# A hybrid layer on one core: five groups of the seven products in w2 of FFN 2, an order of its own for its last part, and softplus among FFN 1's pair jobs

## The chip, the cores and the metric

The kernel runs on one core of one Trainium2 chip. The metric is the time of one execution on the device in microseconds (us). The times shown are of repeated executions of the whole kernel, and the profile is of one more execution of it.

## The reference, cut to what matters

One layer of a streaming encoder for 512 tokens of 1024 channels, in float32. Two feed-forward networks (FFN 1 and FFN 2, hidden width 2816 = 22 tiles of 128) stand around a mixer (a recurrent branch and an attention branch, merged).

```python
def swiglu(x, w1, w3, w2):
    return (jax.nn.silu(x @ w1) * (x @ w3)) @ w2

f = swiglu(rms_norm(h, ffn1_pre_g), ffn1_w1, ffn1_w3, ffn1_w2)
h = h + 0.5 * rms_norm(f, ffn1_post_g)
u = rms_norm(h, mix_pre_g)
...   # recurrent branch: log_a = -8 * r * softplus(-lam), with r a sigmoid; attention; gates
h = h + rms_norm(merged @ w_o, mix_post_g)
f = swiglu(rms_norm(h, ffn2_pre_g), ffn2_w1, ffn2_w3, ffn2_w2)
h = h + 0.5 * rms_norm(f, ffn2_post_g)
```

## The kernel before, in words

**Arithmetic.** Every float32 operand of a product is split into a high part, rounded to the format that TensorE takes, and a low part, the rest. One product is three matmuls: high by high, high by low, low by high. ScalarE makes the high parts, VectorE most of the low ones (a subtraction: `split2`, line 214; `split_to`, line 179).

**w1 and w3 of an FFN: `Pairs`.** The hidden tiles are made two at a time in jobs ("pair jobs", the `run` of `Pairs`, matmuls in lines 683 to 685). Each job computes a 2x2 block product with seven products instead of eight, on sums and differences of blocks: VectorE and POOL make the sums, VectorE and ScalarE split them. `late` is a table of small tasks that are put at marked places (1, 2, 3) of given jobs. `tail()` in the last job prepares the first units of w2.

**w2 of an FFN: `Halves`.** The 22 hidden tiles are the inner dimension. 16 of them, in four groups of four, are multiplied by the same seven-product scheme over halves of the tokens and of the output columns: the products m1, m5, m2, m6, m7, m3, m4 follow one another, and each runs over the four groups. One product of one group is a "unit", u = 0 to 27: twelve matmuls of 128x512 (lines 615 to 617). `prep` makes a unit's operands: a block of w2 (`raw`) is split into `hi` and `lo`, the hidden values into the two parts of `xs`, and then `sums` makes the differences of blocks (`T`, line 548) and of hidden values (`S`, line 551) for later units. Where the low weights come from depends on the product: for m1, m5, m6, m7, m4 VectorE subtracts (line 596); for m2 ScalarE writes the negative of the high part and a DMA issued by POOL adds the weights from HBM to it (line 594); for m3 the high part itself comes by a casting DMA of POOL (line 602), ScalarE writes its negative (line 587) and a POOL DMA adds the weights (line 588).

At step u the program emits the preparation of unit u + 4 (`LEAD = 5`: all units below u + 5), then the hooks of the step, then the unit's matmuls. The first four units are prepared in the last pair job. The hooks load and split the remaining six tiles and read h back. Products that share banks of PSUM are copied out in between (`out`: ScalarE, line 629, after m1, m5 and m6; VectorE's addition, line 627, after m7).

**The rest of w2: `tok_gemm`.** The six tiles left over (`TAIL`) are multiplied classically (`mm_tok`, lines 242 to 244), token tile by token tile and half by half of the output columns, and each token tile is then normed and stored (`post_norm`): an addition where a part lies in a slot (`part`, line 294), the sum of squares by ScalarE (line 298), the gain (line 299), 1/sqrt, and the output (line 310).

**Buffers and order.** SBUF work tiles come from one pool of `NSLOT = 42` slots of 4 KB a partition, given out in the order of the program, so a request waits until an earlier tile of the pool is done with. Loads of weights are queued on SP, broadcasts and adding DMAs on POOL. Each engine takes its instructions in the order in which the program emits them; TensorE runs through units without pause as long as operands are there.

**softplus.** In step 25 of FFN 1's w2 a hook emits softplus(-lam) and three scaled copies of biases: two operations of ScalarE and 28 small ones of VectorE, on 8 to 40 columns (lines 1126 to 1143).

Of the kernel before, what the change touches and what calls it, by code (L numbers as in the profile page):

```python
# [13 lines left out]
ALU = mybir.AluOpType  # L14
# [37 lines left out]
def hybrid_layer(ctx: ExitStack, tc: tile.TileContext, a: dict, out: bass.AP):  # L52
# [65 lines left out]
    want("w2a", TAIL)  # L118
# [16 lines left out]
    want("w2b", TAIL)  # L135
# [148 lines left out]
    def post_norm(acc, t, gpost, scale, dst, after=None, last=False, eps=D * EPS, mid=None, part=None):  # L284

        ss = small(2, "ss")
        fg = slot([P, D], name="fg")
        junk = slot([P, D], name="junk")
        cs = [slice(n * 512, (n + 1) * 512) for n in range(2)]
        if part:  # L290
            acc = list(acc)
            for n, o in enumerate(part):
                if o is not None:
                    dve.tensor_tensor(out=o, in0=acc[n], in1=o, op=ALU.add)
                    acc[n] = o
        rs = Rstd2()
        for n, c in enumerate(cs):
            act.activation(junk[:, c], acc[n], AF.Square, accum_out=ss[:, n : n + 1])
            dve.scalar_tensor_tensor(out=fg[:, c], in0=acc[n], scalar=scale, in1=gpost[:, c], op0=ALU.mult, op1=ALU.mult)
            if n:  # L300
                rs.root(ss)
            else:
                rs.first(ss, eps)
        r = rs.value()
        if mid:
            mid()
        if last:
            cs = [slice(0, 512), slice(512, 768), slice(768, D)]
        for n, c in enumerate(cs):
            dve.scalar_tensor_tensor(out=dst[:, c], in0=fg[:, c], scalar=r, in1=h[t][:, c], op0=ALU.mult, op1=ALU.add)  # L310
            if after:
                after(n, c)

    def norms(acc, t, gpost, scale, gpre, spill, eps, mid=None, part=None):
# [12 lines left out]
        post_norm(acc, t, gpost, scale * NEWT, h[t], half, eps=eps, mid=mid, part=part)  # L327
# [38 lines left out]
    def tok_gemm(nm, xs, n, R, gpost_name, scale, gpre_name, first, x_to=None, xf=None, spill=False, then=None, eps=None, pre=None):  # L366
# [44 lines left out]
        us, trs = {}, {}  # L411
        ep = lambda t: D * EPS if eps is None else eps[:, t : t + 1]
        split_to(st["get"] + len(first))
        dma_to(st["split"] + 2)
        for t in range(NT):
            for ns in ((0,), (1,)):
                for k in tail:
                    new = k == tail[0] and (t > 1 and ns == (1,) if pre else k == 0)
                    mm_tok(accs(t), xs[k], t, w[k], new, k == tail[-1], ns, bool(pre))
            if not gpre_name:  # L420
                o = slot([P, D], name="o")

                def store(nn, c, t=t, o=o):
                    sp.dma_start(out=out[t * P : (t + 1) * P, c], in_=o[:, c])

                post_norm(acc[t], t, gpost, scale * NEWT, o, store, t == NT - 1, part=pre and pre.part(t))
                continue
# [7 lines left out]
            us[t] = norms(acc[t], t, gpost, scale, gpre, spill, ep(t), part=pre and pre.part(t))  # L435
# [22 lines left out]
        us[t] = norms(acc[t], t, gpost, scale, gpre, spill, ep(t), between, pre and pre.part(t))  # L458
# [59 lines left out]
    class Halves:  # L518

        LOADS = tuple((b, i) for bs in (("b11", "b12"), ("b22", "b21")) for i in range(4) for b in bs)  # L520
        NAMES = ("m1", "m5", "m2", "m6", "m7", "m3", "m4")
# [4 lines left out]
        def __init__(self, nm, hid, hooks):  # L526
            self.nm, self.hid, self.hooks = nm, hid, hooks
            self.gs = (1, 2, 3, 4)
# [8 lines left out]
        def load(self, n):  # L537
            while self.loaded < min(n, len(self.LOADS)):
                b, i = self.LOADS[self.loaded]
# [33 lines left out]
        def prep(self, n):  # L573

            while self.ready < min(n, 28):
                u = self.ready
                self.ready += 1
                m, i = self.NAMES[u // 4], u % 4
                self.load(LOAD_AT(u))
# [9 lines left out]
                else:  # L589
                    src = self.raw[b, i]  # L590
                    act.activation(hi, src, AF.Copy)
                    if (m, i) in LO_DMA:
# [6 lines left out]
                if CAST_AT <= u < CAST_AT + 4:  # L599
                    n = u - CAST_AT  # L600
# [4 lines left out]
        def unit(self, u):  # L605
            m = self.NAMES[u // 4]
# [4 lines left out]
            hi, lo, xs = self.ops.pop(u)  # L611
            for j in range(2):
                for t, ps in enumerate(self.bank[key]):
                    c = slice(t * P, (t + 1) * P)
                    pe.matmul(ps, xs[:, 0, j, c], hi[:, j, :], start=start and j == 0, stop=False, skip_group_check=True)
                    pe.matmul(ps, xs[:, 0, j, c], lo[:, j, :], start=False, stop=False, skip_group_check=True)  # L616
                    pe.matmul(ps, xs[:, 1, j, c], hi[:, j, :], start=False, stop=u % 4 == 3, skip_group_check=True)
# [17 lines left out]

        def run(self):
            for u in range(28):
                self.prep(u + LEAD)
                for fn in self.hooks.get(u, ()):
                    fn()  # L640
                self.unit(u)
                if u % 4 == 3 and self.NAMES[u // 4] in ("m1", "m5", "m6", "m7"):
                    later(0, lambda m=self.NAMES[u // 4]: self.out(m), 0)
                point()
# [6 lines left out]
    def blocks(nm, hid, pairs, late, h_src):  # L651

        hooks = {u: [] for u in range(28)}
# [9 lines left out]
        for at_, fn in ((RAW_TAIL, lambda n: dma_to(st["get"] + n + 1)), (SPLIT_TAIL, tail_tile), (H_BACK, h_back)):  # L663
            for n, u in enumerate(at_):
                hooks[u].append(lambda n=n, fn=fn: fn(n))
        half = Halves(nm, hid, hooks)
# [5 lines left out]
        return half  # L672

# [15 lines left out]
    class Pairs:  # L689
# [65 lines left out]
        def run(self, tail, hooks={}):  # L755
# [4 lines left out]
            for n, (nm, f) in enumerate(self.jobs):  # L760
# [23 lines left out]
                if n == len(self.jobs) - 1:  # L784
                    silu()
                    silu = lambda: None
                    tail()
# [18 lines left out]
                if n == len(self.jobs) - 1:  # L806
                    tail()
                    c11()
# [202 lines left out]
    hid, X1 = Hidden(TAIL), {}  # L1011
# [109 lines left out]
    def softplus():  # L1121
        lam = vec[:, V_LAM : V_LAM + KT]
        z = [small(KT, "z", 5) for _ in range(5)]
        act.activation(z[0], lam, AF.Abs)
        act.activation(z[1], z[0], AF.Exp, scale=-1.0)
        dve.tensor_scalar(out=z[2], in0=z[1], scalar1=2.0, scalar2=None, op0=ALU.add)
        dve.reciprocal(z[2], z[2])
        dve.tensor_tensor(out=z[1], in0=z[1], in1=z[2], op=ALU.mult)
        dve.tensor_tensor(out=z[2], in0=z[1], in1=z[1], op=ALU.mult)
        dve.tensor_scalar(out=z[3], in0=z[2], scalar1=1.0 / 17, scalar2=1.0 / 15, op0=ALU.mult, op1=ALU.add)  # L1130
        for c in (13, 11, 9, 7, 5, 3, 1):
            dve.tensor_tensor(out=z[3], in0=z[3], in1=z[2], op=ALU.mult)
            dve.tensor_scalar(out=z[3], in0=z[3], scalar1=1.0 / c, scalar2=None, op0=ALU.add)
        dve.tensor_tensor(out=z[3], in0=z[3], in1=z[1], op=ALU.mult)
        dve.tensor_scalar(out=z[4], in0=lam, scalar1=-1.0, scalar2=0.0, op0=ALU.mult, op1=ALU.max)
        dve.scalar_tensor_tensor(out=z[3], in0=z[3], scalar=2.0, in1=z[4], op0=ALU.mult, op1=ALU.add)
        dve.tensor_scalar(out=chalf, in0=z[3], scalar1=2.0, scalar2=None, op0=ALU.mult)
        dve.tensor_scalar(out=cneg, in0=z[3], scalar1=-4.0, scalar2=None, op0=ALU.mult)
        dve.tensor_scalar(out=bhalf, in0=vec[:, V_BA : V_BG + 16], scalar1=0.5, scalar2=None, op0=ALU.mult)

        for par in range(2):
            for r0 in (0, 64):
                dve.tensor_scalar(
# [78 lines left out]
    for i in range(P // 16):  # L1222
        late[4 + i, 1] = [lambda i=i: bias_spread(i)]

    h.clear()
    half = blocks("w2a", hid, pairs_a, late, lambda t: a["x"][t * P : (t + 1) * P, :])
# [4 lines left out]
    half.hooks[SOFTPLUS_AT].append(softplus)  # L1231
    xf = {(hh, th): slot([P, 4, 256], name="xf") for hh in range(2) for th in range(2)}
    bs = tok_gemm(
        "w2a", hid, FT, len(TAIL), "ffn1_post_g", 0.5, "mix_pre_g", [("xr", i) for i in range(4)], xf=xf, spill=True, eps=veps, pre=half)
# [378 lines left out]
    hid, tn = Hidden(TAIL), []  # L1613
# [33 lines left out]
    t01 = slot([P, 2, SEQ], name="sw")  # L1647
    hid.f[0] = silu_mul(bs[0], bs[1], out=t01[:, 0, :])
    X2["t3"] = to_slots(tn[2])
    hid.f[1] = silu_mul(bs[2], bs[3], out=t01[:, 1, :])  # L1650
    del t01
# [4 lines left out]
    half = blocks("w2b", hid, pairs_b, late, lambda t: h_scr[t])  # L1656
    X2 = pairs_b = None
    tok_gemm("w2b", hid, FT, len(TAIL), "ffn2_post_g", 0.5, None, [], pre=half)
# [27 lines left out]
TAIL = (0, 1, 20, 21, 2, 3)  # L1686
KEPT_AT = (18, 19), (21, 22), (22, 23)
SOFTPLUS_AT = 25
# [10 lines left out]
def LOAD_AT(u):  # L1699
    return min(16, 9 + u)  # L1700
# [62 lines left out]
```

## Time and profile before

| | |
|---|---|
| median of 3 runs | 1110.78 us (1110.55 to 1111.26) |
| the profiled execution | 1110.68 us, span from the first to the last instruction 1108.9 us |
| TensorE (PE) | 1098.4 us busy, mean granted clock 0.998 |
| VectorE (DVE) | 912.5 us busy |
| ScalarE (ACT) | 668.9 us busy |
| GpSimd (POOL) | 389.9 us busy |
| DMA | 155.41 MB, 140 GB/s on average |

A row of the timeline has the start in the span, the duration, the engine, the line of the kernel, the operation, output and inputs by the program's names, the shapes, and in brackets the idle time before it and what ended it. Matmuls are pipelined: the time from one to the next counts, not the duration in the row. A row of the windows has the stretch, its length, and then the busy time and the number of instructions of TensorE, its weight loads, VectorE, ScalarE and POOL, followed by the granted clock, the DMA engines' share and the GB/s.

### The profile page before, as it was taken

To read this page: it belongs to the slowest core of one execution; us is meant where nothing else is said; L and a number is where in the kernel's file an instruction comes from. 1 tells how busy PE (TensorE), PEld (TensorE's weight loads), DVE (VectorE), ACT (ScalarE), POOL (GpSimd) and SP (SyncE) were. 2 spreads that over 40 slices of the span, in tenths; PEclk is the share of its full clock that TensorE was granted. 3 is DMA by queue.
4 is the path that set the end of the run, shared out by engine and by line. 5 is a ranking of instruction groups with operands and counts; after the bars stand their busy time and mean duration, and the time that the engine had idled before them with its cause. 6 is when DMAs were issued, how large, how long until landed. Compare 5 with 4: busy or idle time off the path is not lost.

```text
span 1108.9 us, 17987 instructions
## 1 busy us (share of the span) xinstructions
PE 1098.4 (99%) x6850; PEld 989.6 (89%) x6850; DVE 912.5 (82%) x1337; ACT 668.9 (60%) x1175; POOL 389.9 (35%) x308
## 2 busy tenths in 40 slices
PE   9999999999999999999999999999999999999997
PEld 8899999987879878899888888889999999998885
DVE  5988999999997978887778867767789898689954
ACT  7755555576857678656655654356455555567821
POOL 0143533202212413242656663010976665502100
PEclk9999999999999999999999999999999999999999
DMA  9325663467944642156132435442332323476832
GB/s 338 120 87 140 136 136 115 148 197 159 256 173 186 141 127 79 40 179 239 58 95 77 131 117 223 150 159 95 115 109 83 114 82 110 137 229 148 191 113 76
DMA packets 52662, 155.41 MB, mean 140 GB/s; under 512 B 5456, under 2 KB 7376, under 8 KB 52576
## 3 DMA queue, kind: packets, MB, share of 16 engines
q1 hardware_dynamic: 42256, 129.57, 34.0%
q0 software_dynamic: 10032, 24.16, 11.1%
q8 instruction: 54, 0.88, 0.3%
q10 hardware_dynamic: 288, 0.52, 0.2%
q14 instruction: 32, 0.26, 0.1%
HBM read 138.52 MB, written 13.62 MB: 137 GB/s over the span
## 4 chain that ended last, share of the span: by engine, by line
PE 86%; DVE 10%; DMA 2%; issue 1%; ACT 0%; POOL 0%; DVEq 0%; SPq 0%; POOLq 0%; ACTq 0%
PE c L683 12%; PE c L684 12%; PE c L685 12%; PE f L224 9%; PE f L225 9%; PE f L226 9%; DVE wlo L596 2%; PE acc L243 2%; PE acc L244 2%; PE acc L242 2%; DVE uT L214 1%; DVE raw_w2a L548 1%; PE hw L243 1%; PE hw L244 1%; PE hw L242 1%
## 5 line engine op out<-in xcount | busy, mean ns | idle before, releaser
L684 PE MATMUL c<-uT,wlo 128*128 128x256 f32 x516 | 146.1, 283 | 0.0
L685 PE MATMUL c<-uT,whi 128*128 128x256 f32 x516 | 146.1, 283 | 0.0
L683 PE MATMUL c<-uT,whi 128*128 128x256 f32 x516 | 146.1, 283 | 0.0
L683 PE MATMUL c<-Xh,whi 128*128 128x256 f32 x504 | 142.8, 283 | 0.0
L684 PE MATMUL c<-Xh,wlo 128*128 128x256 f32 x504 | 142.7, 283 | 0.0
L224 PE MATMUL f<-uT,whi 128*128 128x512 f32 (+1 forms) x368 | 136.5, 371 | 0.0
L225 PE MATMUL f<-uT,wlo 128*128 128x512 f32 (+1 forms) x368 | 134.9, 367 | 0.0
L226 PE MATMUL f<-uT,whi 128*128 128x512 f32 (+1 forms) x368 | 134.8, 366 | 0.0
L685 PE MATMUL c<-Xl,whi 128*128 128x256 f32 x456 | 129.1, 283 | 0.0
L214 DVE TENSOR_TENSOR wlo<-S,whi 128x1024 fp32r<-128x1024 f32 x86 | 118.7, 1380 | 8.1 <-POOL OL L1557 4.5
L213 ACT ACTIVATE whi<-S 128x1024 fp32r<-128x1024 f32 x86 | 88.5, 1054 | 31.4 <-DVE S L732 29.7
L684 PEld LDWEIGHTS c<-uT,wlo 128*128 128x128 f32 x516 | 99.1, 192 | 0.2
L683 PEld LDWEIGHTS c<-uT,whi 128*128 128x128 f32 x516 | 99.1, 192 | 0.2
L685 PEld LDWEIGHTS c<-uT,whi 128*128 128x128 f32 x516 | 99.1, 192 | 0.0
L683 PEld LDWEIGHTS c<-Xh,whi 128*128 128x128 f32 x504 | 96.8, 192 | 0.3 <-issue 0.3
L684 PEld LDWEIGHTS c<-Xh,wlo 128*128 128x128 f32 x504 | 96.8, 192 | 0.0
L685 PEld LDWEIGHTS c<-Xl,whi 128*128 128x128 f32 x456 | 87.6, 192 | 0.0
L224 PEld LDWEIGHTS f<-uT,whi 128*128 128x128 f32 x368 | 69.4, 189 | 12.5 <-issue 1.7
L226 PEld LDWEIGHTS f<-uT,whi 128*128 128x128 f32 x368 | 69.4, 188 | 11.4
L225 PEld LDWEIGHTS f<-uT,wlo 128*128 128x128 f32 x368 | 69.5, 189 | 10.8
L1505 POOL TENSOR_SCALAR P<-P,d 128x256 f32<-128x256 f32 (+1 forms) x64 | 62.0, 984 | 45.0 <-DVE d L1503 27.9
L616 PE MATMUL hw<-wlo,uT 128*128 128x512 f32 x192 | 75.2, 392 | 0.4 <-DMA wlo<-in_w2b_dram 0.3
(434 smaller groups left out, 3189.7 us busy)
## 6 DMA issues: line engine op xcount, KB each, us to landing
raw_w2a<-in_w2a_dram SPq DMA_DIRECT2D x22, 512.0 KB, 4.5
raw_w1b<-in_w1b_dram SPq DMA_DIRECT2D x22, 512.0 KB, 4.3
raw_w3b<-in_w3b_dram SPq DMA_DIRECT2D x22, 512.0 KB, 4.3
raw_w2b<-in_w2b_dram SPq DMA_DIRECT2D x22, 512.0 KB, 4.6
raw_w3a<-in_w3a_dram SPq DMA_DIRECT2D x21, 512.0 KB, 4.4
raw_w1a<-in_w1a_dram SPq DMA_DIRECT2D x20, 512.0 KB, 4.5
raw_wg<-in_wg_dram SPq DMA_DIRECT2D x16, 512.0 KB, 4.0
h<-in_x_dram SPq DMA_DIRECT2D x8, 512.0 KB, 6.9
```

What stands on the lines that cost most here:

```text
L213: act.activation(hi, src, AF.Copy)
L214: dve.tensor_tensor(out=lo, in0=src, in1=f32(hi), op=ALU.subtract)
L224: pe.matmul(ps[:, c0:c1], wh[:, s], h_, start=k == 0 and c0 == 0, stop=False, skip_group_check=True)
L225: pe.matmul(ps[:, c0:c1], wl[:, s], h_, start=False, stop=False, skip_group_check=True)
L226: pe.matmul(ps[:, c0:c1], wh[:, s], l_, start=False, stop=k == KT - 1, skip_group_check=True)
L242: pe.matmul(acc[n], x[:, 0, c], wh[:, s], start=first, stop=False, skip_group_check=skip)
L243: pe.matmul(acc[n], x[:, 0, c], wl[:, s], start=False, stop=False, skip_group_check=skip)
L616: pe.matmul(ps, xs[:, 0, j, c], lo[:, j, :], start=False, stop=False, skip_group_check=True)
L683: pe.matmul(ps, wh[:, s], xh, start=first, stop=False, skip_group_check=True)
L684: pe.matmul(ps, wl[:, s], xh, start=False, stop=False, skip_group_check=True)
L685: pe.matmul(ps, wh[:, s], xl, start=False, stop=k == 3, skip_group_check=True)
L1505: pool.tensor_scalar(out=pt[:, x, b0:256], in0=pt[:, x, b0:256], scalar1=d[:, x : x + 1], scalar2=None, op0=ALU.mult)
```

## The change

**FFN 2's w2.** Five groups instead of four go through the seven products (20 of 22 tiles, 35 units); two tiles (20 and 21) stay classical. The order of the products becomes m1, m5, m2, m6, m3, m7, m4, and the blocks are loaded in another order. `last_gemm` replaces `tok_gemm` there. It runs the units of m1, m5, m2, m6 and m3 (0 to 24), then the classical tiles of the first two token tiles and their norms, then m7's units, then the classical tiles of the second column half of token tiles 2 and 3, then m4 for token tile 2 alone, its first half's classical tiles and its norm, and the same for token tile 3. Within the last two norms the column half with an addition is taken first. The five units of m2 and of m3 still get their low parts by DMA. Four units are prepared in the last pair job, as before. The gain is broadcast at step 20, and h is read back at steps 19, 20, 26 and 28.

**FFN 1's w2** keeps its four groups and its order; token tiles 2 and 3 take their column halves in the other order, in matmuls and norms, and in the last pair job the third prepared unit is emitted after the last product but two, not before.

**softplus** is emitted in pair jobs 12 to 16 of FFN 1: two operations on ScalarE in job 12, three on VectorE in job 13, and the rest as 28 small operations of POOL in jobs 13 to 16. Step 25 of the w2 stage has none of it any more.

```diff
-    def post_norm(acc, t, gpost, scale, dst, after=None, last=False, eps=D * EPS, mid=None, part=None):
+    def post_norm(acc, t, gpost, scale, dst, after=None, last=False, eps=D * EPS, mid=None, part=None, ns=(0, 1)):
...
-        if part:
-            acc = list(acc)
-            for n, o in enumerate(part):
-                if o is not None:
-                    dve.tensor_tensor(out=o, in0=acc[n], in1=o, op=ALU.add)
-                    acc[n] = o
         rs = Rstd2()
-        for n, c in enumerate(cs):
-            act.activation(junk[:, c], acc[n], AF.Square, accum_out=ss[:, n : n + 1])
-            dve.scalar_tensor_tensor(out=fg[:, c], in0=acc[n], scalar=scale, in1=gpost[:, c], op0=ALU.mult, op1=ALU.mult)
-            if n:
+        for j, n in enumerate(ns):
+            c, x, o = cs[n], acc[n], part and part[n]
+            if o is not None:
+                dve.tensor_tensor(out=o, in0=x, in1=o, op=ALU.add)
+                x = o
+            act.activation(junk[:, c], x, AF.Square, accum_out=ss[:, j : j + 1])
+            dve.scalar_tensor_tensor(out=fg[:, c], in0=x, scalar=scale, in1=gpost[:, c], op0=ALU.mult, op1=ALU.mult)
+            if j:
                 rs.root(ss)
...
     class Halves:
-        NAMES = ("m1", "m5", "m2", "m6", "m7", "m3", "m4")
...
+            self.G = G = len(gs)
+            self.loads = [(b, i) for bs in (("b11", "b12"), ("b22", "b21")) for i in range(G) for b in bs]
+            if G > 4:
+                self.loads[2 * G :] = [(b, i) for b in ("b22", "b21") for i in range(G)]
+            self.cast_at = names.index("m3") * G - 5
...
-                self.load(LOAD_AT(u))
+                self.load(min(4 * G, 2 * G + 1 + u))
...
+    def last_gemm(nm, hid, half, gpost_name, scale):
+        tail, G, w = list(hid.seq), half.G, {}
+        gpost = []
+        half.hooks[GPOST_AT].append(lambda: gpost.append(bcast(gpost_name)))
+        for u in range(5 * G):
+            half.step(u)
...
+        for t in range(2):
+            for n in range(2):
+                classical(t, n)
+            half.prep(5 * G + LEAD + 1 + t)
+            norm(t, (0, 1))
+        for u in range(5 * G, 6 * G):
+            half.step(u)
+        for t in range(2, 4):
+            acc[t] = [half.bank["bu"][t - 2], bank("acc")]
+            classical(t, 1, True)
+        for t in range(2, 4):
+            for u in range(6 * G, 7 * G):
+                half.step(u, (t - 2,))
+            classical(t, 0)
+            norm(t, (1, 0), t == 3)
...
+    def softplus_out():
+        pool.tensor_scalar(out=chalf, in0=z[3], scalar1=2.0, scalar2=None, op0=ALU.mult)
...
+    late[12, 1], late[13, 1] = [softplus_exp], [softplus_ratio]
+    late[13, 3], late[14, 2] = [lambda: softplus_terms((13, 11, 9))], [lambda: softplus_terms((7, 5))]
+    late[15, 2], late[16, 2] = [lambda: softplus_terms((3, 1))], [softplus_out]
...
-TAIL = (0, 1, 20, 21, 2, 3)
+TAIL_A = (0, 1, 20, 21, 2, 3)
-CAST_AT = 15
-LO_DMA = {("m2", i) for i in range(4)}
-RAW_TAIL = (14, 16, 18, 20, 22, 24)
-SPLIT_TAIL = (16, 18, 20, 22, 24, 26)
-H_BACK = (24, 25, 26, 27)
+GS_A = (1, 2, 3, 4)
+NAMES_A = ("m1", "m5", "m2", "m6", "m7", "m3", "m4")
+MARKS_A = (14, 16, 18, 20, 22, 24), (16, 18, 20, 22, 24, 26), (24, 25, 26, 27)
+TAIL_B = (20, 21)
+GS_B = (0, 1, 2, 3, 4)
+NAMES_B = ("m1", "m5", "m2", "m6", "m3", "m7", "m4")
+MARKS_B = (13, 15), (17, 19), (19, 20, 26, 28)
+GPOST_AT = 20
```

More of the change, by code (lines that the diff above doesn't have):

```diff
@@ L457, in tok_gemm @@
         mm_feat(bs[0], ws[0], 0, 256, ks=range(3, KT))
-        us[t] = norms(acc[t], t, gpost, scale, gpre, spill, ep(t), between, pre and pre.part(t))
+        us[t] = norms(acc[t], t, gpost, scale, gpre, spill, ep(t), between, pre and pre.part(t), halves(t))
         transpose_out(trs[t - 1], t - 1, parts=(1,))
@@ L672, in blocks, with classical, norm, store @@
         return half
+    def last_gemm(nm, hid, half, gpost_name, scale):
[4 more added lines that the diff above has]
+            half.step(u)
+        for i, k in enumerate(tail):
+            w[k] = get(nm, k, ahead=len(tail) - 1 - i, rawahead=0)
+        acc = {t: [half.bank["bc"][t], half.bank["bx"][t]] for t in range(2)}
+        def classical(t, n, new=False):
+            for k in tail:
+                mm_tok(acc[t], hid[k], t, w[k], new and k == tail[0], k == tail[-1], (n,), True)
+        def norm(t, ns, last=False):
+            o = slot([P, D], name="o")
+            def store(nn, c):
+                sp.dma_start(out=out[t * P : (t + 1) * P, c], in_=o[:, c])
+            post_norm(acc[t], t, gpost[0], scale * NEWT, o, store, last, part=half.part(t), ns=ns)
+        for t in range(2):
[13 more added lines that the diff above has]
+            norm(t, (1, 0), t == 3)
     QH = 4 * P
```

147 lines of the change are left out of this document (77 added, 70 removed).

## The prediction

> **What bounds the kernel now.** I read the page first, then the waits of TensorE, then the timeline of TensorE, VectorE, ScalarE and the DMA issues in the three places that the change touches: the w2 stage of FFN 2, the w2 stage of FFN 1, and the end.
>
> ```profile
> span 1108.9 us, 17987 instructions
> ...
> PE 1098.4 (99%) x6850; PEld 989.6 (89%) x6850; DVE 912.5 (82%) x1337; ACT 668.9 (60%) x1175; POOL 389.9 (35%) x308
> PEclk9999999999999999999999999999999999999999
> PE 86%; DVE 10%; DMA 2%; issue 1%; ACT 0%; POOL 0%; DVEq 0%; SPq 0%; POOLq 0%; ACTq 0%
> ```
>
> TensorE is busy for 1098.4 of 1108.9 us at a granted clock of nine tenths or more in every slice, and it carries 86% of the chain that ended last. So a matmul taken out saves its step, a wait of TensorE costs its full length, and work of other engines counts where TensorE waits for it, or behind its last matmul. The step comes from two rows of the timeline near the end, 54 matmuls apart; the other rows are the end itself.
>
> ```profile
> 1088.68 0.39 PE L244 MATMUL hw<-whi,hT 128*128 128x512 f32 x1
> 1089.11 0.60 ACT L298 ACTIVATE junk<-hw 128x512 f32<-128x512 f32 x1 [2.30 <-PE hw L244]
> 1089.60 0.19 ACT L298 ACTIVATION_READ_ACCUMULATOR junk<-hw 128x1 f32 x1
> ...
> 1100.92 0.39 PE L244 MATMUL acc<-whi,hT 128*128 128x512 f32 x1
> ...
> 1103.21 0.21 DVE L260 TENSOR_SCALAR v<-ss,b 128x1 f32<-128x1 f32 x1
> 1104.08 1.54 DVE L310 SCALAR_TENSOR_TENSOR o<-fg,r,h 128x512 f32<-128x512 f32 x3
> ```
>
> (1100.92 - 1088.68) / 54 = 0.2267 us for a 128x512 step.
>
> **The change part by part.**
>
> **1. Matmuls.** Four tiles done classically cost 4 tiles x 4 token tiles x 2 halves x 3 = 96 matmuls; as a fifth group of the seven products they cost 7 x 12 = 84. Twelve go: 12 x 0.2267 = **-2.72 us**, all of it on the path.
>
> **2. VectorE in m1 and m5.** This is the price of part 1. A unit takes TensorE 12 x 0.2267 = 2.72 us. In the m1 and m5 products VectorE does four operations for each unit: the low part of the weights, the low part of the hidden values, a weight difference, a hidden sum.
>
> ```profile
> 999.00:1035.00 36.00, 35.90 (x157) 28.88 (x155) 36.00 (x44) 24.85 (x33) 7.73 (x8) 1.00 0.63 148
> ```
>
> ```profile
> 1005.40 1.22 DVE L596 TENSOR_TENSOR wlo<-raw_w2b,whi 128x1024 fp32r<-128x1024 f32 x1
> ...
> 1008.88 1.21 DVE L596 TENSOR_TENSOR wlo<-raw_w2b,whi 128x1024 fp32r<-128x1024 f32 x1
> 1010.01 0.68 DVE L214 TENSOR_TENSOR uT<-hEO,uT 128x512 fp32r<-128x512 f32 x1
> ...
> 1012.35 0.68 DVE L214 TENSOR_TENSOR uT<-hEO,uT 128x512 fp32r<-128x512 f32 x1
> ```
>
> ```profile
> 1009.77 0.39 PE L615 MATMUL hw<-whi,uT 128*128 128x512 f32 x1
> 1010.14 0.50 PE L616 MATMUL hw<-wlo,uT 128*128 128x512 f32 x1
> 1010.75 0.50 PE L617 MATMUL hw<-whi,uT 128*128 128x512 f32 x1
> ```
>
> The first fence is a window: its third busy column is VectorE, 36.00 of 36.00 us without a gap. The second shows its rhythm: 1008.88 - 1005.40 = 3.48 us for an m5 unit, 1012.35 - 1010.01 = 2.34 us from the last m5 unit's low values to those of the first m2 unit. The third is the last of the eight m1 and m5 units: its second matmul starts as the low weights end (1008.88 + 1.21 = 1010.09) and its third as the low values end (1010.01 + 0.68 = 1010.69). TensorE waited (0.37 - 0.23) + (0.61 - 0.23) = 0.52 us: four units prepared in the last pair job, and the four-unit lead, were just used up. The change makes it ten units, and nothing in it takes an operation of these units off VectorE or starts them earlier: still four units are prepared in FFN 2's last pair job. Each of the two added units is then paced by VectorE: 2 x (3.48 - 2.72) = **+1.52 us**. In m2 and m6 a unit costs VectorE 2.34 us against 2.72, so it gains 0.38 a unit and later units aren't held up by it. Bounds: +0.8 if one unit of lead is found, +2.2 if ScalarE or a slot adds a few tenths to each.
>
> **3. m3 moved ahead of m7.** Today m7 follows m6 on the same banks and has to wait for ScalarE's copy of them:
>
> ```profile
> 1034.68 0.39 PE L617 MATMUL hw<-whi,uT 128*128 128x512 f32 x1
> 1035.08 0.50 PE L615 MATMUL hw<-whi,uT 128*128 128x512 f32 x1
> ```
>
> 0.40 - 0.23 = 0.17 us. With m3 between them, on other banks, it goes: **-0.2**. After m7 the copy moves to VectorE's addition, and m4 follows on the same banks; but the two classical half-tiles put there are 12 x 0.2267 = 2.7 us of matmuls, and two additions are some 1.4 us (twice the 0.68 us of a 128x512 operation of VectorE, above). Nothing late.
>
> **4. Low parts made by DMA.** In m2 and m3 ScalarE writes the negative and a POOL DMA adds the weights. Five units each instead of four. The timeline of the last m3 unit today, then ScalarE and POOL at m3's first unit, then the two landing lines (m3, m2):
>
> ```profile
> 1054.25 0.39 PE L615 MATMUL hw<-whi,uT 128*128 128x512 f32 x1
> 1054.98 0.50 PE L616 MATMUL hw<-wlo,uT 128*128 128x512 f32 x1 [0.34 <-DMA wlo<-in_w2b_dram]
> 1055.32 0.39 PE L617 MATMUL hw<-whi,uT 128*128 128x512 f32 x1
> ```
>
> ```profile
> 1034.43 1.28 ACT L629 ACTIVATE hc<-hw 128x512 f32<-128x512 f32 x2 [2.55 <-PE hw L617]
> 1035.60 1.05 ACT L587 ACTIVATE wlo<-whi 128x1024 fp32r<-128x1024 f32 x1
> 1036.95 1.22 POOL L588 DMA_DIRECT2D wlo<-in_w2b_dram  x1 [9.27 <-ACT wlo L587]
> ```
>
> ```profile
> DMA to landing us min/median/max: 6.0/7.9/10.7
> DMA to landing us min/median/max: 6.4/7.0/7.2
> ```
>
> Today's price is (0.73 - 0.23) + (0.34 - 0.23) = 0.61 us. In the new order the copy of m6's banks stands, on ScalarE, ahead of the fifth m3 unit alone (it is emitted behind step 19, that unit's preparation in step 20). Count from the end of m6: the row of the copy began 0.48 us before m6's end (1034.68 + 0.23), so it ends at +0.80; the negative to +1.8; POOL's DMA starts 0.30 after it, +2.1; it lands at +8.1, +10.0 or +12.8 (min, median, max). TensorE needs it four units later, at 4 x 2.72 + 0.23 = +11.1. By the median it is in time. But buffers are short there. By the code, in step 20 the pool of 42 slots is asked for 10 of hidden values, 15 raw blocks (m7 comes last, and until then five each of b11, b22 and b21 are kept), 3 copies, 6 for the two classical tiles, 10 operands of m3, 2 of h and 1 gain: 47; the same count today at m3's steps is about 30. If the negative waits for the slots of one more unit, all moves by 2.72: median +12.7, 1.6 us late. Between 0 and 1.6, and with h loads and the gain broadcast beside it, I take 1.1, that is **+0.5** against today. Ends: -0.6 (in time) and +3.8 (latest landing and a unit's wait, 15.5 - 11.1 - 0.6). The fifth m2 unit stands behind the m5 copy in the same way, with one 1.05 us cast more: lands at +9.5 to +10.3 by the m2 line. In time: 0. SP's queue has the same 22 loads of w2, but two instead of six stand behind the blocks; the h loads come earlier and delay nothing that is queued behind them.
>
> **5. The end.** The norm of the last tile now takes the half that needs an addition first, while TensorE still works. Today, behind the last matmul's start at 1100.92: v is computed at +2.29 and the output begins at +3.16; an addition and both gains come before v. A half without an addition is seen at 1089.11: the square starts 0.43 us behind its matmul and its sum is read by +1.11; a gain of 0.68 us begun at +0.43 ends there too. So v can start at +1.16 and the output at +2.03, **-1.1 us** (bounds -0.9 and -1.2). The norms of the first two tiles run beside m7's 13.6 us; VectorE has some 5 us of norm each there and only single units of 1.7 us queued behind.
>
> **6. softplus.** Today it sits on VectorE ahead of the last split of FFN 1's w2 tail.
>
> ```profile
> 306.63 0.16 DVE L1126 TENSOR_SCALAR z<-z 128x8 f32<-128x8 f32 x1
> ...
> 313.45 1.22 DVE L179 TENSOR_TENSOR wlo<-raw_w2a,whi 128x1024 fp32r<-128x1024 f32 x1
> ```
>
> ```profile
> 313.67 0.39 PE L242 MATMUL hw<-whi,hT 128*128 128x512 f32 x1
> 314.73 0.50 PE L243 MATMUL hw<-wlo,hT 128*128 128x512 f32 x1 [0.67 <-DVE wlo L179]
> ```
>
> Its operations stand between the two rows, with one 0.7 us split of hidden values behind them. Without them that split starts at 306.63, and the low weights are there by 306.63 + 0.7 + 1.22 = 308.5, five us ahead of need: 1.06 - 0.23, **-0.8 us**. Next on VectorE are the splits of xr, which nobody needs before the tail ends. Its new place is the pair jobs:
>
> ```profile
> 60.00:222.00 162.00, 162.00 (x1349) 161.53 (x1349) 144.99 (x180) 89.75 (x146) 60.45 (x38) 1.00 0.49 130
> ```
>
> ```profile
> 188.03 2.32 DVE L214 TENSOR_TENSOR wlo<-S,whi 128x1024 fp32r<-128x1024 f32 x1
> ```
>
> TensorE is never idle there; ScalarE (89.75) and POOL (60.45 of 162) have room for the two table switches and 28 small operations. Beside POOL's adds a VectorE split took 2.32 instead of 1.22 us, so POOL's work isn't free for VectorE. The 28 have 8 or 40 columns; at 0.2 us (an estimate, just above the 0.16 of VectorE's row of 8 columns) they are 5.6 us over four jobs, at most 2 us in one, against VectorE's idle (162 - 145) / 162 x 10 = 1.0 us a job. I take 0 for TensorE and keep +1.4 as the other end: 5.6 less four jobs' idle, carried into FFN 1's m5, where VectorE sets the pace.
>
> The Trainium skill, "SBUF — State Buffer", section "SBUF: two separate sides", says that the two engines share one pair of ports under an exclusive lock, and that the loser stops until the other's whole instruction is over. The 2.32 us row agrees; by that rule the whole 5.6 us would be VectorE's, which is rival three below.
>
> Moving FFN 1's third prepared unit behind the last products changes no operation of VectorE, which from 224 to 253 us is the pacing engine there as here; 0. The other edits of the norms reorder work beside matmuls; 0.
>
> **Sum:** -2.72 + 1.52 - 0.2 + 0.5 - 1.1 - 0.8 = -2.8. The profiled execution took 1110.68 us (span 1108.9), the median is 1110.78: 1110.78 - 2.8 = **1108.0 us**.
>
> **The rivals.**
> One, nothing made by DMA is late: m3's wait is gone, 1.1 less, and the lead helps m5: 1106.0 to 1106.9. For: the median landings. Against: 47 requests for 42 slots.
> Two, slots decide, and it gets slower: from the point where the fifth m3 unit's negative gets its slot three units late (h and gain taken first): +2.1 + 8.16 + 7.9 = +18.2, 7.1 us late, 6.0 more than taken: 1114.0. For: five slots too few, five such requests in steps 19 and 20. Against: the two units freed first suffice for those queued ahead of it.
> Three, softplus on POOL stops VectorE and lengthens FFN 1's m5: +1.4, 1109.4. For: the 2.32 us row. Against: POOL is idle for most of a job.
> Four, parts 2 and 4 both come at their upper ends (+0.7, +1.6): 1110.3, no difference.
>
> **How the numbers follow.** A measurement of this kernel tells some 0.2%, 2.2 us, from no change: faster ends at 1108.6, slower begins at 1113.0. Forecast 0.48, with a range of its own from 1107.0 to 1109.2, of which an eighth lies above 1108.6: 0.42 faster, 0.06 same. Rival one 0.16, faster. Rival two 0.13: it has one place and one price, but it is where the code asks for more than there is; slower. Three 0.10, of which 0.02 faster. Four 0.13, same. Faster 0.60, same 0.27, slower 0.13. The range from 1106.0 to 1111.0 leaves out rival two and the edges of the others, below 2 in 10.
>
> **What would show it.** Twelve 128x512 matmuls fewer; TensorE waiting about 2 us in all in the last two m5 units, behind VectorE's low parts 3.48 us apart; no 0.17 us gap behind m6; the wait for the last m3 unit's DMA near 1 us; output about 2.0 us behind the last matmul; no wait at the last tile of FFN 1's tail. Wrong would be: m5 without a longer wait (VectorE got lead from somewhere), m3 waits of several us (slots), or longer waits in FFN 1's m5 (POOL).

## The result, and the profile after

| | median (range, runs) | ratio to the kernel before, 95% interval |
|---|---|---|
| before | 1110.78 us (1110.30 to 1111.26, 6) | |
| after | 1125.20 us (1123.76 to 1128.67, 6) | 1.0135 [1.0125, 1.0146] |

The change made the kernel slower by 14.4 us, where 2.8 us faster was forecast. The profiled execution took 1123.97 us, with a span of 1122.2, which is 13.3 more than before. The page of the kernel after: engines, granted clock in 40 slices, chain.

```profile
PE 1100.6 (98%) x6838; PEld 988.0 (88%) x6838; DVE 923.3 (82%) x1323; ACT 675.8 (60%) x1183; POOL 408.4 (36%) x339
PEclk9999999999999999999999999999999999999998
PE 81%; DVE 10%; ACT 3%; issue 3%; DMA 3%; POOL 0%; DVEq 0%; SPq 0%; POOLq 0%; ACTq 0%
```

Twelve matmuls fewer (6838 against 6850), and yet TensorE is busy 2.2 us longer; the last slice has a lower clock. What TensorE waited for (us in total, times, the longest):

```profile
PE hw L619 <- DVE hc L631: 8.3, 1, 8.3
PE hw L620 <- DMA wlo<-in_w2b_dram: 2.7, 4, 0.8
...
PE tr L341 <- DVE hg L331: 1.0, 1, 1.0
```

One wait carries most of it: m4's first matmul (line 619) waits for VectorE's addition (line 631) that empties m7's banks. TensorE's timeline there, and two windows, the second over the nine matmuls behind the wait:

```profile
1088.12 0.39 PE L244 MATMUL acc<-whi,hT 128*128 128x512 f32 x1
1096.78 0.77 PE L619 MATMUL hw<-whi,uT 128*128 128x512 f32 x1 [8.27 <-DVE hc L631]
1097.34 0.63 PE L620 MATMUL hw<-wlo,uT 128*128 128x512 f32 x1
...
1100.33 0.57 PE L621 MATMUL hw<-whi,uT 128*128 128x512 f32 x1
1100.74 0.40 PE L619 MATMUL hw<-whi,uT 128*128 128x512 f32 x1
```

```profile
1063.00:1096.00 33.00, 24.67 (x108) 20.01 (x107) 30.84 (x44) 18.25 (x29) 0.00 (x0) 0.92 0.19 67
1096.78:1100.33 3.55, 3.55 (x9) 2.81 (x9) 3.48 (x5) 0.72 (x2) 0.00 (x0) 0.50 0.14 55
```

TensorE stood still for 8.66 - 0.23 = 8.4 us, and the nine matmuls behind it ran at a granted clock of 0.50: 3.96 us for 9 x 0.2267 = 2.04, another 1.9. In the first window VectorE is busy 30.84 of 33.00 us. What it does (VectorE's timeline):

```profile
1062.76 1.23 DVE L598 TENSOR_TENSOR wlo<-raw_w2b,whi 128x1024 fp32r<-128x1024 f32 x1 [4.34 <-PE hw L620]
...
1078.88 0.68 DVE L294 TENSOR_TENSOR hc<-hw,hc 128x512 f32<-128x512 f32 x1
...
1087.18 0.68 DVE L294 TENSOR_TENSOR hc<-hw,hc 128x512 f32<-128x512 f32 x1
...
1091.14 1.42 DVE L308 SCALAR_TENSOR_TENSOR o<-fg,r,h 128x512 f32<-128x512 f32 x2
...
1095.95 1.28 DVE L631 TENSOR_TENSOR hc<-hw,hc 128x512 f32<-128x512 f32 x2
```

It waited until 1062.76 for a unit of TensorE, prepared m7's five units and one of m4's until 1078.88, normed the first token tile, prepared another m4 unit, normed the second tile (1087.18 to 1092.5), prepared two more m4 units, and only then came to the addition. TensorE's last m7 matmul had been issued by 1085.6.

The other places: the last m3 unit waits for its DMA (three units before it do the same), an m5 unit waits for VectorE, and the end.

```profile
1062.73 0.39 PE L619 MATMUL hw<-whi,uT 128*128 128x512 f32 x1
1063.96 0.50 PE L620 MATMUL hw<-wlo,uT 128*128 128x512 f32 x1 [0.84 <-DMA wlo<-in_w2b_dram]
```

```profile
1014.87 0.39 PE L619 MATMUL hw<-whi,uT 128*128 128x512 f32 x1
1015.35 0.50 PE L620 MATMUL hw<-wlo,uT 128*128 128x512 f32 x1
1015.95 0.50 PE L621 MATMUL hw<-whi,uT 128*128 128x512 f32 x1
```

```profile
1114.80 0.39 PE L244 MATMUL hw<-whi,hT 128*128 128x512 f32 x1
1115.72 0.19 ACT L296 ACTIVATION_READ_ACCUMULATOR junk<-hw 128x1 f32 x1
1115.94 0.69 DVE L297 SCALAR_TENSOR_TENSOR fg<-hw,bc_ffn_post_g 128x512 f32<-128x512 f32 x1 [3.72 <-ACT junk L296]
1117.42 1.54 DVE L308 SCALAR_TENSOR_TENSOR o<-fg,r,h 128x512 f32<-128x512 f32 x3
```

By steps of TensorE beyond 0.2267 us, the two traces differ so: matmuls -2.7; m5 +1.5 (2.2 against 0.7); m6's copy -0.3; m3 +3.1 (3.7 against 0.6); m4's wait +8.4 and the slow matmuls +1.9; the end -0.6 (7.4 us behind the last matmul's start against 8.0); FFN 2's w2 starts 1.7 later (992.4 against 990.7). The sum is 13.0 of the 13.3.

### The profile page after: what moved, and what is told of

It is laid out like the page before. It is cut to its first block, busy times and chain, and to the rows that moved or that the text cites. A ratio compares the mean times of both kernels' runs of the same rounds, so it can differ in the third digit from the quotient of the medians.

```text
span 1122.2 us, 17986 instructions
## 1 busy us (share of the span) xinstructions
PE 1100.6 (98%) x6838; PEld 988.0 (88%) x6838; DVE 923.3 (82%) x1323; ACT 675.8 (60%) x1183; POOL 408.4 (36%) x339
## 4 chain that ended last, share of the span: by engine, by line
PE 81%; DVE 10%; ACT 3%; issue 3%; DMA 3%; POOL 0%; DVEq 0%; SPq 0%; POOLq 0%; ACTq 0%
PE c L731 12%; PE c L730 12%; PE c L732 12%; PE f L224 9%; PE f L225 9%; PE f L226 9%; PE hw L620 2%; PE hw L621 2%; PE hw L619 2%; DVE wlo L598 2%; DMA wlo<-in_w2b_dram 1%; PE acc L244 1%; PE acc L242 1%; PE acc L243 1%; DVE raw_w2b L549 1%
## 5 line engine op out<-in xcount | busy, mean ns | idle before, releaser
L619 PE MATMUL hw<-whi,uT 128*128 128x512 f32 x220 | 86.7, 394 | 8.3 <-DVE hc L631 8.3
L620 PE MATMUL hw<-wlo,uT 128*128 128x512 f32 x220 | 87.7, 399 | 3.2 <-DMA wlo<-in_w2b_dram 2.7
L621 PE MATMUL hw<-whi,uT 128*128 128x512 f32 x220 | 87.0, 396 | 0.5
```

## The experiments

Theory one: VectorE's queue makes m4 wait, since norms and preparations stand ahead of the addition. Theory two: what is emitted ahead of m3's operands (slots for classical tiles, h, gain) makes m3 late, and with it VectorE. For FFN 1: softplus, the column order, or the norms' new order of operations.

**1. Norms behind m7's addition**, on the kernel after:

```diff
-            norm(t, (0, 1))
         for u in range(5 * G, 6 * G):
             half.step(u)
+        for t in range(2):
+            norm(t, (0, 1))
```

> The kernel after, with the norms of token tiles 0 and 1 emitted behind m7's units and the addition that empties m7's banks, instead of ahead of them. Theory one (VectorE's queue): m4's first matmul waited 8.4 us for that addition because the two norms (1078.9 to 1085.5 and 1087.2 to 1092.6) stand ahead of it on VectorE. Without them VectorE has four m4 units of about 1.8 us behind the last m7 unit (1078.9), so the addition ends near 1087.4, ahead of 1088.3: the 8.4 us and the 1.9 us of half-speed matmuls behind it go: 1125.2 - 10.3 = about 1115. Rival (VectorE is late already, by the slots that it waited for until 1062.8): part of the wait stays, or it comes back at the end, where the last norm now stands behind three others: 1119 to 1123.

Measured 1121.82 us, 1.0105 [1.0091, 1.0119]. The waits of TensorE:

```profile
PE hw L619 <- ACT uT L213: 3.9, 1, 3.9
PE hw L620 <- DMA wlo<-in_w2b_dram: 3.7, 4, 1.7
...
PE hw L620 <- DVE wlo L598: 0.9, 1, 0.9
```

The wait for the addition is gone. But the last m4 unit is prepared at step 30, which is now emitted behind the norms: a new wait in place of the old one. The number lies in the rival's range by luck, not by the rival's mechanism.

**2. Requests behind m3**, on the kernel after:

```diff
-MARKS_B = (13, 15), (17, 19), (19, 20, 26, 28)
-GPOST_AT = 20
+MARKS_B = (20, 20), (23, 24), (24, 24, 26, 28)
+GPOST_AT = 24
```

> The kernel after, with the loads and splits of the two classical tiles, the first two loads of h and the gain emitted behind the preparation of the last m3 unit (steps 20 to 24 instead of 13 to 20), so that m3's operands get their slots first. Theory two (42 slots are too few at m3): m3's waits for the adding DMAs, 3.7 us in all, fall below 1 us, VectorE starts on m7's operands some 4 us earlier, and the 8.4 us wait of m4 shrinks by as much: 1116 to 1119. If only the latency of the adding DMAs makes m3 late, m3's waits stay at 3 to 4 us: 1124 to 1126. If the slots do and m4's wait hangs on the norms alone: 1121 to 1123.

Measured 1115.12 us, 1.0042 [1.0029, 1.0056]. The waits:

```profile
PE hw L243 <- DVE wlo L179: 2.8, 1, 2.8
...
PE hw L620 <- DMA wlo<-in_w2b_dram: 0.3, 1, 0.3
```

The time is a little under theory two's 1116 to 1119. Of m3's waits 0.3 us is left, and that part of theory two is shown: it is what was emitted ahead of m3, not the latency of the DMAs as such. Slots and ScalarE's casts of the classical tiles moved together here, so this run doesn't tell the two apart. The kernel after speaks for the slots: ScalarE stood idle ahead of m3's third negative and of the copy of m6's banks, until VectorE had split a classical tile (line 179), which is when that tile's block of weights is done with. ScalarE's timeline there:

```profile
1048.65 1.06 ACT L589 ACTIVATE wlo<-whi 128x1024 fp32r<-128x1024 f32 x1 [1.29 <-DVE wlo L179]
...
1054.77 1.09 ACT L633 ACTIVATE hc<-hw 128x512 f32<-128x512 f32 x2 [1.29 <-DVE wlo L179]
```

There is no wait at m4 in run 2 either, but the second classical tile's low part came 2.8 us late, with 8 slow matmuls behind it (1.5 us), so TensorE reached m4 late itself.

**3 and 4. FFN 1's parts alone**, on the kernel before: softplus among the pair jobs; and the column order of the tail with the norms' new order of operations.

> The kernel before, with softplus alone moved to the pair jobs. Theory: the wait of 0.83 us in FFN 1's w2 tail goes, but POOL's small operations and the two moved ones hold VectorE up by some 0.7 us in the pair jobs, which FFN 1's m5 passes on: 1110.5 to 1111.0. Rival (VectorE's 0.7 us come from something else): 1109.9 to 1110.1. Rival two (it also makes the adding DMAs of FFN 1's m3 late, 0.8 us): 1111.5.

> The kernel before, with the other column order of token tiles 2 and 3 in FFN 1's w2 tail alone (matmuls and norms; the addition of each half now stands just ahead of its own square and gain in all norms). Theory: the gain of the half without an addition waits for the square of the same bank, and the norms of tiles 2 and 3 end 1.2 us later, which the transposes of the last tile pass on to TensorE: 1111.8 to 1112.2. Rival (the shift of the transposes comes from the later m3 alone): 1110.6 to 1111.0.

Softplus alone: 1110.56 us, 1.0000 [0.9991, 1.0009], no difference. The wait of 0.8 us in the tail is gone, but VectorE is 0.6 us later from that stretch of the pair jobs on. In the profiled execution FFN 1's m3 also waited 1.6 us for its DMAs, but at 1111.98 us that execution was the slowest of the eleven, so the median needn't have this wait. Column order: 1112.14 us, 1.0015 [1.0006, 1.0024], +1.9, as the theory had it; which of its two edits does it was still open (12).

**5. Splits at steps 22 and 23**, otherwise as 2:

> As the run with the loads, splits, h and gain behind m3's preparation, but the two classical tiles are split at steps 22 and 23 instead of 23 and 24. That run had no wait at m4 and 0.3 us at m3, but TensorE waited 2.8 us for the second tile's low part and ran 8 matmuls at half speed behind that (1.6 us). Theory (slots are what made m3 and then VectorE late): both go, no new wait takes their place: 1115.1 - 4.4 = 1110.7. Rival (the norms' place alone matters, and the 8.4 us wait at m4 was hidden by the wait ahead of it): the wait at m4 comes back with 2 to 4 us: 1112 to 1115.

Measured 1117.11 us, 1.0056 [1.0042, 1.0070]: slower than 2. The wait at m4 came back, as the rival had it (4.2 us, for its 2 to 4), though the time lies above the rival's range.

```profile
PE hw L619 <- DVE hc L631: 4.1, 1, 4.1
```

```profile
1051.00:1089.00 38.00, 33.85 (x147) 27.06 (x145) 35.60 (x49) 22.52 (x35) 1.56 (x2) 1.00 0.45 135
```

In 2 the addition began at 1088.11 and TensorE came at 1089.2; here it began at 1088.59, but TensorE was there at 1085.2 and waited. VectorE is busy 35.60 of the 38 us ahead of it; its longest wait there is 1.40 us, for ScalarE inside the first norm. So theory one stands by itself: even with m3 in time, the work that the order puts ahead of the addition is too long, by 4.2 us, with 1.4 us of slow matmuls behind it. In 2 the earlier wait only hid that.

**6 and 7. FFN 1 as before but for the norms' order of operations; and, on top, m1's low weights of units 3 and 4 by DMA** (`if m == "m2" or (m, G) == ("m1", 5) and i > 2`), both on 5:

> The same with FFN 1 as in the kernel before (column order of the tail, place of the third prepared unit, softplus in the w2 stage): what is left is the five groups and the last part of FFN 2. The column order alone cost 1.9 us and softplus's new place 0.3 us on the kernel before. Theory (the parts add): 1110.7 - 2.0 = 1108.7 with a range of 1108.2 to 1109.3, which is faster than the kernel before by 12 matmuls (2.7), less two units paced by VectorE (1.5), less the gain at the end (0.6) . Rival (FFN 1's parts cost nothing here): 1110.5.

> The same, and the low weights of the last two m1 units of FFN 2 come by ScalarE's negative and an adding DMA of POOL, as m2's do: 2 x 1.2 us less for VectorE ahead of m5. Theory (VectorE paces m5): its waits of some 2.2 us in units 7 to 9 fall to 0.3 or less and the time by 1.5 to 2: 1106.7 to 1107.2. Rival (the wait moves to the new DMAs, 7 us from issue to landing, or ScalarE is late): no change, or up to 2 us slower.

Measured 1118.53 us, 1.0064 [1.0051, 1.0077], and 1117.77 us, 1.0061 [1.0048, 1.0074]. Neither time is near its theory. In 6 the transposes of FFN 1 still waited (1.6 us), with the column order of before: the order isn't what costs. In 7 m5's waits for VectorE are gone, a wait of 1.2 us for unit 4's DMA came, and the wait at m4 stayed at 4.1, so what m5 gained could not be seen whole.

**8. All m4 units prepared ahead of the norms**, on 1 (`half.prep(7 * G)` ahead of them):

> The run with the two norms behind m7's addition had no wait for m4's banks any more, but the last m4 unit was still prepared behind the norms: TensorE waited 3.9 us for its hidden values and 0.9 us for its low part and more, and ran slow behind it. Here all m4 units are prepared ahead of the norms; m3's late slots stay. Theory (the norms ahead of the addition, and nothing else, made m4 wait, once VectorE was late): these waits go, 1121.8 - 6 - 1.5 = 1114 to 1115, and m3's 4 us stay. Rival (VectorE has too much work before the end whatever the order): a wait of 3 us or more comes back at the norms of the last tiles, 1118 or more.

Measured 1117.29 us, 1.0056 [1.0042, 1.0069].

```profile
PE hw L620 <- DMA wlo<-in_w2b_dram: 4.5, 3, 3.6
```

No wait is left at m4, as theory one says. The time lies between the theory's 1114 to 1115 and the rival's 1118. In the profiled execution one of m3's DMAs was so late (3.6 us) that 14 matmuls behind it ran slow; but that execution was the slowest of the four (1115.29 to 1118.71 us), so how much of this stands in the median is not shown.

**9. Both moves** (5 and 8 together), and **10. with FFN 1 as in the kernel before**, additions first:

```diff
+        if part:
+            acc = list(acc)
+            for n, o in enumerate(part):
+                if o is not None:
+                    dve.tensor_tensor(out=o, in0=acc[n], in1=o, op=ALU.add)
+                    acc[n] = o
         rs = Rstd2()
```

> Both moves together: loads, splits, h and gain behind m3's preparation, splits at steps 22 and 23, and the norms of token tiles 0 and 1 behind all of m4's preparations and m7's addition. Each alone left one wait: the first a wait of 4.2 us for VectorE's addition and 1.8 us of slow matmuls (1117.1), the second the waits at m3. Theory (two causes: slots make m3 late, and VectorE's work ahead of the addition is too long whatever the slots do): neither wait is there, 1117.1 - 6.0 = 1111.1. Rival (VectorE's work only moves to the end): the last norm starts late and 1114 or more.

> The same with FFN 1 as in the kernel before: its column order, its prepared units, softplus in the w2 stage, and all additions of a norm ahead of its squares and gains. FFN 2 started 1.4 us later in the run with the splits two steps on (992.1) than in the kernel before (990.7). Theory (it is the additions' place, not the column order, that FFN 1 loses by): it starts at 990.7 again and the time is 1111.1 - 1.4 = 1109.7, within 0.2% of the kernel before: 12 matmuls less (2.7), two more units paced by VectorE (1.5), a gain of 0.6 at the end. Rival (something else in FFN 1): FFN 2 starts above 992, 1111.

Measured 1112.12 us, 1.0014 [1.0005, 1.0023], and 1109.40 us, 0.9991 [0.9982, 0.9999]. Both are near the theory's 1111.1 and 1109.7: 9 is 0.1% slower than the kernel before, 10 is 0.1% faster. In 10, TensorE's waits of over 0.5 us by this view are two:

```profile
PE w L1042 <- POOL warm L1039: 1.1, 1, 1.1
PE hw L243 <- DVE wlo L179: 0.8, 1, 0.8
```

The first is the start of every run, the second is for the second classical tile's low part (1.1 us by its steps). FFN 2's w2 starts at 990.5, against 990.7 before.

**11. m1's units 2 and 3 by DMA**, on 10:

> The same, and the low weights of m1's units 2 and 3 of FFN 2 come by ScalarE's negative and an adding DMA. With units 3 and 4 the waits of m5 (2.2 us) were gone but unit 4's DMA was 1.2 us late; one unit earlier each should be in time. Theory (VectorE paces m5): 1109.7 - 2.0 = 1107.7, faster than before. Rival (the DMA is late again, or VectorE's rest is enough to pace): 1108.7 or more.

Measured 1110.03 us, 0.9994 [0.9985, 1.0003]: no difference from 10 that its interval can tell, as the rival had it. m5's waits are gone, but unit 3's DMA was 1.0 us late.

**12. The additions' place alone**, on the kernel before:

> The kernel before with one change in the norms: each addition stands just ahead of its own square and gain, not both ahead of all. Column order, softplus and FFN 2's scheme are as before. Theory (VectorE's gain of the half without an addition waits for ScalarE's square of the same bank, and the other half's addition now stands behind it): the last tile's transposes in FFN 1 wait some 1.1 us, 1111.5 to 1112.2, as in the run with the column order, whose cost then isn't the order's. Rival (the column order): 1110.4 to 1110.9.

Measured 1112.20 us, 1.0017 [1.0008, 1.0026], the same as 4: the place of the additions costs the 1.9 us, the column order nothing beside it. VectorE in the norm of FFN 1's last tile, in the kernel before and in this run, and TensorE's wait in this run:

```profile
345.90 0.69 DVE L294 TENSOR_TENSOR hc<-acc,hc 128x512 f32<-128x512 f32 x1
346.51 0.68 DVE L299 SCALAR_TENSOR_TENSOR fg<-hw,bc_ffn_post_g 128x512 f32<-128x512 f32 x1
```

```profile
347.57 0.69 DVE L297 SCALAR_TENSOR_TENSOR fg<-hw,bc_ffn_post_g 128x512 f32<-128x512 f32 x1 [0.57 <-ACT junk L296]
348.18 0.20 DVE L256 TENSOR_SCALAR b<-ss,veps 128x1 f32<-128x1 f32 x1
348.30 0.68 DVE L294 TENSOR_TENSOR hc<-acc,hc 128x512 f32<-128x512 f32 x1
```

```profile
PE tr L341 <- DVE hg L331: 1.6, 2, 1.1
```

The gain of the first half waits for ScalarE's square, which reads the same bank, and the other half's addition, on another bank, stands behind it. Before, the addition stood first and filled that time. By the start of FFN 2's w2 this has cost 2.5 us (993.2 against 990.7); behind it the profiled execution is 1.0 us shorter, 0.6 of it because m3's DMA was in time there and 0.4 at the end. The Trainium skill, "PSUM — Partial Sum Buffer", section "PSUM bank collisions raise a hardware error", wants two engines' reads of one bank kept apart; these traces agree: the gain starts at 347.57, when ScalarE's read of the sum has ended at 347.54.

**13 and 14. One m1 unit (2), and units 1 and 2, by DMA**, both classical tiles split at step 22, on 10:

> The run with FFN 1 as before, both classical tiles split at step 22 (the second tile's low part was 1.0 us late there), and the low weights of one m1 unit of FFN 2, unit 2, by ScalarE's negative and an adding DMA. Theory (m5 is paced by VectorE, 1.2 us are taken off it; of two units in a row only the second DMA was late): m5's waits go from 2.3 to 1.1 us and the split's wait goes: 1109.4 - 2.2 = 1107.2. Rival (what m5 gains is waited for later, since VectorE paces the whole stretch to m7's addition): 1108.4.

> The same with units 1 and 2 by DMA, each a step earlier than where the second was late. Theory: m5's waits of 2.3 us go, and both DMAs are in time: 1109.4 - 3.3 = 1106.1. Rival (the second of two adding DMAs is late whichever units they belong to, by the 1.0 to 1.2 us seen twice, because w2's loads take the DMA engines then): 1107.2.

Measured 1108.37 us, 0.9978 [0.9968, 0.9987], and 1108.77 us, 0.9981 [0.9972, 0.9990]. Both beat the kernel before, by 0.2%. 13 has the lowest time here, though not one that can be told from 14's, and it gains 1.0 us on 10, not its theory's 2.2. It meets the rival's number, 1108.4, by luck: VectorE doesn't make TensorE wait again behind m5; DMAs do. 14 meets neither of its two numbers. In 13:

```profile
PE hw L623 <- DMA wlo<-in_w2b_dram: 1.7, 2, 1.2
```

Even a single adding DMA came late (unit 2, 1.5 us by its steps, 9.7 us from issue to landing), and so did one of m3's (0.7). The 2.2 us of m5 and the 1.1 at the split are gone, and these 2.2 stand in their place: 1.1 in all, against the 1.0 measured. In 14 a DMA of m1's and one of m3's were late by 1.1 us each. That VectorE alone paces m5 is shown by 7, 11, 13 and 14, where a low part or two less on it left no wait for it; most of the gain is taken back by DMAs.

## Why the prediction was wrong

**The step that failed** is the sentence in part 5 that the norms of the first two tiles run beside m7's matmuls, with only single units of 1.7 us behind them, and with it "Nothing late" in part 3. It priced each of VectorE's pieces against TensorE's and never added up the queue ahead of the addition on which m4's banks hang: m7's five preparations and the first of m4's (1062.76 to 1078.88, 16.1 us), two norms (6.6 and 5.3) and three more m4 units (5.2). The window of VectorE that was quoted stops at 1035; in the stretch where the change put all this, the kernel before and the kernel after show

```profile
1065.00:1090.00 25.00, 25.00 (x112) 20.71 (x111) 9.25 (x20) 5.46 (x13) 0.00 (x0) 1.00 0.08 31
1065.00:1090.00 25.00, 23.51 (x104) 19.14 (x102) 23.09 (x32) 11.45 (x19) 0.00 (x0) 1.00 0.06 22
```

9.25 us of VectorE's 25 against 23.09. It cost 8.4 us, and 1.9 more for the clock, which the prediction had no term for. Runs 5 and 8 show the cause from both sides: with m3 in time a wait of 4.2 us is left, with the norms behind the addition none. The rest of the 8.4 us is m3's lateness, which kept VectorE until 1062.76 (part 4), and with both moved (run 9) 13.1 of the 14.4 us are gone.

**1, matmuls:** right, -2.7. **2, VectorE in m5:** right: +1.5 said, +1.5 measured, waits of 0.7 us in each of the two added units as described. **3:** the gap behind m6 went (-0.3 for -0.2). **4, m3:** right in part. +0.5 was taken from a range of -0.6 to +3.8, and +3.1 measured. The shortage that it named was there, but it hit four of the five units, not the last alone, and the issues came late, not the landings (6.2 to 8.6 us after issue, 6.0 to 10.7 in the kernel before). For the last unit the prediction has POOL's DMA start 2.1 us behind m6's end, or one unit of 2.72 us later; it started 8.4 behind it (1057.48 against 1049.05), since the copy of m6's banks ahead of it on ScalarE began only at 1054.77. With the requests emitted behind m3 (run 2) it started 2.0 behind m6's end (1050.30 against 1048.26), as counted, and the waits fell to 0.3 us. Rival two named this place and the right sign, but its price (one unit 7 us late) isn't what happened: no unit was over 1.1 us late. m3's lateness mattered most by holding VectorE until 1062.76. **5, the end:** -0.6 for -1.1. The last half's gain doesn't run beside its square, but behind it: it starts at 1115.94, when the sum has been read, and the output comes 2.6 us behind the last matmul, not 2.0. **6, softplus:** -0.8 said, 0 measured on its own. The wait at the tail went, but it wasn't a fixed 0.8 us. With softplus in step 25 as before, the same step waits 0.1 us in the profiled execution of run 12 and 0.5 us in that of 13, where TensorE comes to it later (at 314.38 and 314.08 against 313.67). And POOL's 28 operations are not 0.2 us each: they took 17.0 us, not 5.6. Their two largest groups (busy us, mean ns):

```profile
L1191 POOL TENSOR_SCALAR z<-z 128x8 f32<-128x8 f32 x7 | 4.3, 619 | 0.6
L1190 POOL TENSOR_TENSOR z<-z,z 128x8 f32<-128x8 f32 x7 | 3.9, 563 | 0.4
```

VectorE was 0.6 us later in FFN 1's m5 (41.64 us from a split ahead of this stretch, at 170.12, to one behind it, at 211.76; 41.03 in the kernel before). 0.2 of that stood before POOL's first operation, so not all of it is POOL's, and the runs don't divide it further. Rival three had this place, with 1.4. **"The other edits of the norms reorder work beside matmuls; 0"** failed by 1.9 us (run 12): they stand on the path at the last tile of FFN 1, where TensorE waits for the transposes.

With these waits taken away, the sum closes: the profiled execution of run 10 lies 1.8 us under that of the kernel before by its span (1107.1 against 1108.9), from -2.7 of matmuls, +1.5 of m5, -0.3 and -0.6 of the waits behind m6 and in m3, +1.1 of the late split, -0.6 at the end and -0.2 by which FFN 2's w2 started earlier. That execution was the fastest of run 10's eleven; by all of them the gain is about 1 us (0.9991 [0.9982, 0.9999]).

## What to carry to other kernels

Before work is moved to a place "beside matmuls", add up everything that the engine's queue holds there ahead of the one operation that frees a bank or a buffer, over the whole stretch, and compare it with TensorE's time to that point; a view by windows gives it in one line. Emit the operation that frees banks, and the preparations that TensorE needs next, ahead of work that nobody waits for, such as norms and stores; and where buffers are short, let the requests that are needed first come first. Removing one wait can uncover the next (run 5 took away run 2's wait of 2.8 us and was slower), so read where the pacing engine stands, not only where TensorE stands.

## What the runs showed of the hardware

**A long wait costs more than its length.** Behind TensorE's waits of 2.8 us and more matmuls took 0.43 us a step instead of 0.2267 for some 3 to 6 us, 1.4 to 3 us extra each time: nine matmuls in the kernel after and 14 in run 8, at a granted clock of 0.50, and eight in run 2. Behind waits of up to 1.7 us (run 1) no step was longer for it. The Trainium skill, "TensorE: Matmul & The Clock Gate", section "Part 1: The HAM clock gate", has the clock fall to half after an idle window of about 3.4 us and come back after as much work. The traces agree in kind; a wait of 2.8 us was enough here.

**Small POOL operations are not cheap beside VectorE.** On 8 columns they took 0.20 to 1.21 us, with means near 0.6, where VectorE's own took 0.16 to 0.2. The 28 took 17.0 us, and VectorE came 0.6 us later through them, so POOL was held up more than VectorE. The Trainium skill, "SBUF — State Buffer", section "SBUF: two separate sides", has whichever of the two starts first keep the shared ports for its whole instruction, against VectorE operations with two SBUF inputs among others, while the other one is blocked. That leaves this outcome open; no row here names what a POOL operation waited for.

**Adding DMAs of 512 KB** landed 5.5 to 13.3 us after their issue in FFN 2's w2 stage (5.5 in run 2, 13.3 in run 14). In run 13 an issue 8.4 us ahead of need was too late: that one took 9.7 us.
